# A hybrid decoder step on one Trainium2 core: gate temporaries beside the mixing get a buffer of their own, and the output projection's banks are copied before their squares are taken

## The chip, the cores and the metric

The kernel runs on one core of a Trainium2 chip. TensorE multiplies and writes its sums into banks of PSUM (512 fp32 columns on 128 partitions each); ScalarE (ACT), VectorE (DVE) and GpSimd (POOL) move and transform data between PSUM and SBUF; SyncE (SP) and ScalarE's queue issue the DMAs between SBUF and DRAM. Each engine runs its own instructions in order and waits on semaphores for the others. The metric is the device time of one execution in microseconds, and lower is better. The time before is the median of three runs.

## What is computed

One layer of a decoder, for a prompt of 1024 tokens and a sample group of 64 tokens (8 sequences of 8) that share the weights. Model width is 1024, the feed-forward width 2816:

```python
def swiglu(x, w_gu, w_down):
    g, u = jnp.split(x @ w_gu, 2, axis=-1)
    return (jax.nn.silu(g) * u) @ w_down
...
        x = x + 0.5 * rms_norm(swiglu(rms_norm(x, norm_ffn1_pre[l]), ffn1_w_gu[l], ffn1_w_down[l]),
                               norm_ffn1_post[l])
        h = rms_norm(x, norm_mix_pre[l])
        z = h @ w_in[l] + b_in[l]
        q, k, v, hq, hf, hi, hg = jnp.split(z, [int(c) for c in np.cumsum(IN_SPLITS)[:-1]], axis=-1)
...
        mix = jnp.concatenate([a, o], axis=-1) @ w_out[l]
        x = x + rms_norm(mix, norm_mix_post[l])
        x = x + 0.5 * rms_norm(swiglu(rms_norm(x, norm_ffn2_pre[l]), ffn2_w_gu[l], ffn2_w_down[l]),
                               norm_ffn2_post[l])
```

Here `a` is a windowed attention with sinks, normalised, and `o` a chunked gated linear recurrence (HGRN2), normalised and gated. So the order of the layer is: first FFN, mixing (input projection, attention and recurrence, output projection), second FFN.

## The kernel before

The 1088 tokens are split into three groups: group 0 with 320 columns (256 prompt tokens and the 64 sample tokens), groups 1 and 2 with 384 prompt tokens each. Every large product is made in three matmuls (`mm3`, L279 to L281) of operands split into a high and a low part: hi x hi, hi x lo, lo x hi. A weight tile is loaded into a `raw` slot (three of them), cast to its high part on ScalarE (L258, `wsph`) and subtracted to its low part on VectorE (L259, `wspl`); eight tiles of tag `wsp` hold four such pairs. Products go into `mm` banks (four), small ones of the mixing into `ax` banks (four).

The FFN for group 0 is done column tile by column tile. A unit (`up0`) makes the gate bank, 24 matmuls of 320 columns, and the up bank, 24 more. `gated0` copies the gate bank to a temporary (L676), applies Silu to it (L677), multiplies it by the up bank on VectorE (L680) and stores it to DRAM from SyncE's queue (L681). Before, this temporary is one of the eight tiles of tag `t2` (`tmp2`), 128 x 512 fp32 each, which rotate among all temporaries of the mixing (attention probabilities and their transposes, the recurrence's Q, K and D, gain rows, loaded residual rows).

The mixing is woven into the large products: `mixer(n)` is a generator, started as a stream, and each unit of a large product calls `tick()`, which advances the streams by their rates. Group 0 is ready for the second FFN first, so its units are placed among the rest: five head units at the end of group 1's mixing, then group 2's mixing starts, and beside it stand the output projection of group 1 and nine more head units; the output projection of group 2 follows. `need(name)` writes out what is left of a stream. Then eight more head units run, with the stream that adds the residual of group 2 (`post_n`) and prepares its FFN input (`pre_s`). The written order is not final: a scheduler with a time line of its own reorders each engine's instructions when the program is built, so that an instruction's place on its engine follows from when that time line has its inputs and buffers ready.

The output projection of groups 1 and 2 (`w_out_units`, the loop over two column halves `hf`) makes three banks of 128 tokens x 512 columns from four weight tiles. ScalarE then squares each bank with a sum along the row (for the norm, L1535) and copies it to `y` in SBUF (L1537); VectorE multiplies `y` in place by the gain row (L1539). A bank is free for the next product when its square and its copy are done. As each group has two halves, there are 12 squares and 12 copies in all.

Other lines that the prediction's steps touch: the mixing's transposes and products on TensorE are L1154, L1178, L1206, L1219 (attention), L1251, L1274, L1305, L1323, L1329, L1332, L1336 (recurrence); L1195 is the attention's exponential and L1325 the copy of the recurrence's transposed keys, both on ScalarE; L1239 copies K into a temporary; L1413 stores a piece of the sample group's attention; L1307, L1141 and L1142 form the last part of the mixing's output, whose high and low parts the output projection reads.

Of the kernel before, what the change touches and what calls it, by code (L numbers as in the profile page):

```python
# [8 lines left out]
F32 = mybir.dt.float32  # L9
# [4 lines left out]
AF = mybir.ActivationFunctionType  # L14
# [4 lines left out]
P = 128  # L19
D = 1024  # L20
# [17 lines left out]
Z_K, Z_V, Z_HQ, Z_HF, Z_HI, Z_HG = 4, 5, 6, 10, 14, 18  # L38
LEVELS = [64, 32, 16, 8, 4, 2, 1]
NRAW = 3  # L40
WARM = 23, 7
P1 = 1.4

# [2 lines left out]
def tile_step(ctx: ExitStack, tc: tile.TileContext, A: dict, O: list):  # L46
    nc = tc.nc
    V, S, G, PE = nc.vector, nc.scalar, nc.gpsimd, nc.tensor
# [8 lines left out]
    def uid(s):  # L57
        cnt[0] += 1
        return f"{s}_{cnt[0]}"

    def mmbank():
        return ps.tile([P, 512], F32, tag="mm", bufs=4, name=uid("mm"))
# [8 lines left out]
    def big(dt=F32, shape=(P, 4, 384)):  # L71
        return pp.tile(list(shape), dt, tag="big", bufs=12, name=uid("big"))
# [17 lines left out]
    def rawslot(shape=(P, KC, P)):  # L90
        return pp.tile(list(shape), F32, tag="raw", bufs=NRAW, name=uid("raw"))

# [4 lines left out]
    def stream(name, gen, rate):  # L97
        streams[name] = [gen, rate, 0.0]

    def tick():  # L100
        for name in list(streams):
            st = streams[name]
            st[2] += st[1]
            while st[2] >= 1.0:
                st[2] -= 1.0
                if next(st[0], "end") == "end":
                    del streams[name]
                    break
# [12 lines left out]
    junk = cp.tile([P, 512], BF16, name="junk")  # L121
# [132 lines left out]
    def small():  # L254
        return pp.tile([P, 4, 8], F32, tag="small", bufs=10, name=uid("sm"))
# [5 lines left out]
    def load_w(src, pool, tag, bufs, shape=(P, KC, P)):  # L261

        raw = rawslot(shape)
        for sl, ap in src:
            nc.sync.dma_start(raw if sl is None else raw[:, :, sl], ap)
        hi = pool.tile(list(shape), F32R, tag=tag, bufs=bufs, name=uid(tag + "h"))
        lo = pool.tile(list(shape), F32R, tag=tag, bufs=bufs, name=uid(tag + "l"))
        split(hi, lo, raw)
        return hi, lo
# [4 lines left out]
    def load_up(w, c0):  # L274
        return load_w([(None, wsrc(w, c0))], pp, "wsp", 8)
# [7 lines left out]
    def hcol(h, k, w):  # L283
        return h[0][k // 4][:, k % 4, :w], h[1][k // 4][:, k % 4, :w]

    def proj(out, wt, h, w, ks=range(KC)):
        for k in ks:
            mm3(out, (wt[0][:, k, :], wt[1][:, k, :]), hcol(h, k, w), k == 0, k == KC - 1)

    def proj_tok(banks, wt, h, n, ks):  # L290

        for i, bank in enumerate(banks):
            r = rows_of(n, i)
            for k2, k in enumerate(ks):
                hh = hcol(h, k, WIDTH[n])
                mm3(bank[:r], (hh[0][:, i * P:i * P + r], hh[1][:, i * P:i * P + r]),
                    (wt[0][:, k2], wt[1][:, k2]), k == 0, k == KC - 1)
# [8 lines left out]
    def tmp2(name, shape=(P, 512)):  # L306
        return pp.tile(list(shape), F32, tag="t2", bufs=8, name=uid(name))
# [96 lines left out]
    def gain_row(ap, scale, hf):  # L404
        g = tmp2("gb")
        nc.scalar.dma_start(g, ap[0:1, hf * 512:hf * 512 + 512].partition_broadcast(P))
        if scale is not None:
            V.tensor_scalar(g, g, scale, None, op0=ALU.mult)
        return g
# [146 lines left out]
    def pre_first(y, rows, gpre, h, raws, wts, part):  # L556
# [7 lines left out]
        def warm(n):  # L564
            for _ in range(n):
                last = PE.matmul(spare[:, :P], ones, ones, start=True, stop=True).ins
            return last

        last_tr = warm(WARM[0])
        V.memset(sm[:, 0, :], 1.0)  # L570
# [22 lines left out]
        for d in range(KC):  # L593
            bank = axbank("tr")
            with tc.issue_after(last_tr):
# [5 lines left out]
                if d == 1:  # L601
                    last_tr = warm(WARM[1])
            hi, lo = hcol(hx, d, w)
# [44 lines left out]

    def make_ffn(wgu, wdn, h, tag):
        f = FFN()  # L650
        f.SF, f.ys, f.pool = {}, {}, None
        acts = dr.tile([P, NJ, WIDTH[0]], F32, name=f"act{tag}")
        FA = dr.tile([P, NK, 7, 384], F32, name=f"fa{tag}")
        FB = dr.tile([P, NK, 4, 512], F32, name=f"fb{tag}")
# [16 lines left out]

        def gated0(j, g):
            w = WIDTH[0]
            t = tmp2("sg")

            S.copy(t[:, :w], g[:, :w])  # L676
            S.activation(t[:, :w], t[:, :w], AF.Silu)  # L677

            def rest(u):
                V.tensor_tensor(t[:, :w], t[:, :w], u[:, :w], op=ALU.mult)  # L680
                return nc.sync.dma_start(acts[:, j], t[:, :w]).ins  # L681
            return rest
# [360 lines left out]
    def mixing(tp, h):  # L1043
# [464 lines left out]
        def w_out_units(n, ys, sums):  # L1508
            w = WIDTH[n]
            if n == 0:  # L1510
                y = ys[n] = [big(), big()]
                for d in range(KC):
                    wt = load_up(w_out, d * P)
                    bank = mmbank()
                    proj(bank[:, :w], wt, MT[n], w, range(4))
                    tick()
                    proj(bank[:, :w], wt, MT[n], w, range(4, 8))
                    S.copy(y[d // 4][:, d % 4, :w], bank[:, :w])
                    tick()
                return  # L1520
            y = ys[n] = [big(F32, (P, 3, 512)), big(F32, (P, 3, 512))]
            sm = sums[n] = small()
            wts = Ahead([lambda kk=kk, hf=hf: load_w([(None, w_out[
                kk * 256:(kk + 1) * 256, hf * 512:hf * 512 + 512].rearrange("(k p) m -> p k m", p=P))],
                pp, "wsp", 8, (P, 2, 512)) for hf in range(2) for kk in range(4)])
            for hf in range(2):
                banks = [mmbank() for _ in range(3)]
                for kk in range(4):
                    wt = wts.next()
                    proj_tok(banks, wt, MT[n], n, (2 * kk, 2 * kk + 1))  # L1530
                    tick()
                    tick()
                g = gain_row(A["norm_mix_post"], None, hf)
                for i in range(3):
                    S.activation(junk, banks[i], AF.Square, scale=D ** -0.5,  # L1535
                                 accum_out=sm[:, 0, 4 * hf + i:4 * hf + i + 1])
                    S.copy(y[hf][:, i], banks[i])  # L1537
                for i in range(3):
                    V.tensor_tensor(y[hf][:, i], y[hf][:, i], g, op=ALU.mult)  # L1539

# [3 lines left out]
    def seq(*gens):  # L1544
        for g_ in gens:
            yield from g_
# [68 lines left out]
    f2 = make_ffn(A["ffn2_w_gu"][0], A["ffn2_w_down"][0], hffn2, 2)  # L1615
# [3 lines left out]
    def done_mix(n):  # L1619
        y, g = ym[n], cols[:, C_F2PRE:C_F2PRE + 8]  # L1620
        if n == 0:
            stream("c0", seq(post_t(y, x1T, cols[:, C_MPOST:C_MPOST + 8], x2T), pre_t(y, g, hffn2)), RB0)
        else:
            stream(f"c{n}", seq(post_n(n, y, sums[n], x1N[n - 1]),
                                pre_s(n, y, g, part, f2.SF, x2N[n - 1])), RB1)

    with tc.tile_pool(name="mx", bufs=1) as tp:
        w_in_units, mixer, w_out_units = mixing(tp, hmix)
        need("c0")
        w_in_units(0)  # L1630
        stream("m0", mixer(0), RM[0])
        half1(1)
        f1.pair(PB, False, last=lambda: f1.begin_pair((7,), False))
        done1(1)
        f1.pair((7,), False, last=lambda: f1.begin_pair((4,), False))
        half1(2)
        f1.pair((4,), False)
        done1(2)
        need("c1")
        w_in_units(1)  # L1640
        need("m0")
        stream("m1", mixer(1), RM[1])
        w_out_units(0, ym, sums)
        done_mix(0)
        need("c2")
        w_in_units(2)
        need("c0")
        f2.head(range(HEAD2[0]))
        need("m1")
        stream("m2", mixer(2), RM[2])  # L1650
        w_out_units(1, ym, sums)
        done_mix(1)
        f2.head(range(HEAD2[0], HEAD2[1]))
        need("c1")
        need("m2")
        w_out_units(2, ym, sums)
        done_mix(2)
    def out0():
        y = f2.ys[0]
        yield from post_t(y, x2T, halfpost[:, 8:16])  # L1660
        for i in range(3):
            r = rows_of(0, i)
            dst = O[0][0, i * P:(i + 1) * P] if r == P else O[1].rearrange("b t d -> (b t) d")
            for hf in range(2):
                bank = axbank("yo")
                for c in range(4):
                    PE.transpose(bank[:r, c * P:(c + 1) * P], y[hf][:, c, i * P:i * P + r], ident)
                o = tmp2("yo")
                S.copy(o[:r], bank[:r])
                nc.sync.dma_start(dst[:, hf * 512:hf * 512 + 512], o[:r])  # L1670
            yield
# [37 lines left out]
    with tc.tile_pool(name="f2", bufs=1) as tp:  # L1709
# [10 lines left out]
        y, sm = f2.ys[1], small()  # L1720
# [32 lines left out]
```

## Time and profile before

| | us |
|---|---|
| median of 3 runs | 1993.24 (1992.93 to 1993.47) |
| the profiled execution | 1993.22 |
| span of its instructions | 1991.5 |
| TensorE busy | 1978.7 |
| VectorE busy | 1406.9 |
| ScalarE busy | 949.0 |
| GpSimd busy | 178.0 |

An engine's busy time is the union of its instructions' spans; idle time of an engine is shown in square brackets in a timeline, with what released it. In a list of waits the three numbers are us in all, times, and the longest. In a list of groups they are the busy time, the mean ns of one and the idle time just before them. Matmuls overlap, so that TensorE's pace is read from the distance between starts, not from the length of one.

### The profile page before, as it was taken

The numbers are of one execution on the slowest core, as the hardware profiler recorded it, in microseconds if no ns is written. First come the engines' busy times: TensorE is split into PE (matmuls) and PEld (weight loads), VectorE is DVE, ScalarE is ACT, GpSimd is POOL, SyncE is SP. The second block draws the span as 40 slices with busy tenths as digits, with TensorE's granted clock in tenths as the row PEclk, the third lists the DMA queues.
The fourth block names the chain that finished last, engine by engine and source line by source line (L and its number), as shares of the span: only waits on it lengthen the run. The fifth ranks groups of instructions, "written<-read, shape, count | busy, mean of one in ns | idle before, by whom it ended". The sixth has DMA issues, their size and how long they took to land.

```text
span 1991.5 us, 34618 instructions
## 1 busy us (share of the span) xinstructions
PE 1978.7 (99%) x13331; PEld 1854.6 (93%) x13331; DVE 1406.9 (71%) x2595; ACT 949.0 (48%) x1736; POOL 178.0 (9%) x244
## 2 busy tenths in 40 slices
PE   9999999999999999999999999999999999999998
PEld 8999999999998987797999898989999999999886
DVE  7686767886558656777667756756887877655667
ACT  5753334444445444445344444756544444444453
POOL 0000000000004101211113311220000000000201
PEclk9999999999999999999999999999999999999999
DMA  8735555755677647766434343527565555677874
GB/s 230 225 107 186 175 170 177 232 196 192 228 243 212 182 138 236 251 169 181 128 104 132 92 138 107 177 90 237 165 210 191 197 183 193 209 232 232 291 262 140
DMA packets 377319, 370.31 MB, mean 186 GB/s; under 512 B 40546, under 2 KB 294321, under 8 KB 377137
## 3 DMA queue, kind: packets, MB, share of 16 engines
q1 hardware_dynamic: 371169, 357.21, 56.9%
q10 hardware_dynamic: 5984, 10.88, 1.6%
q8 instruction: 105, 1.72, 0.4%
q14 instruction: 61, 0.50, 0.1%
HBM read 284.31 MB, written 84.71 MB: 185 GB/s over the span
## 4 chain that ended last, share of the span: by engine, by line
PE 96%; DMA 1%; DVE 1%; ACT 1%; issue 0%; SPq 0%; DVEq 0%; ACTq 0%
PE mm L279 28%; PE mm L280 28%; PE mm L281 28%; PE pv L1219 1%; PE c L281 1%; PE c L279 1%; PE c L280 1%; PE sc L1178 1%; PE pT L1206 1%; PE tr L511 1%; DMA ar<-fa 1%; PE lv L1251 1%; PE l L1274 0%; DMA raw<-in_ffn_w_gu_dram 0%; DMA xt<-in_x_prompt_dram 0%; PE av L1329 0%
## 5 line engine op out<-in xcount | busy, mean ns | idle before, releaser
L279 PE MATMUL mm<-h,wsph 128*128 128x320 f32 (+1 forms) x1280 | 407.3, 319 | 0.0
L280 PE MATMUL mm<-h,wsph 128*128 128x320 f32 (+1 forms) x1280 | 405.3, 317 | 0.0
L281 PE MATMUL mm<-h,wspl 128*128 128x320 f32 (+1 forms) x1280 | 403.6, 317 | 0.0
L258 ACT CAST wsph<-raw 128x1024 fp32r<-128x1024 f32 x200 | 209.1, 1048 | 269.6 <-PE mm L280 213.7
L259 DVE TENSOR_TENSOR wspl<-raw,wsph 128x1024 fp32r<-128x1024 f32 x200 | 247.7, 1240 | 125.3 <-ACT wsph L258 120.7
L258 ACT CAST w<-raw 128x512 fp32r<-128x512 f32 (+1 forms) x218 | 160.3, 740 | 209.2 <-PE mm L280 111.9
L259 DVE TENSOR_TENSOR w<-raw,w 128x512 fp32r<-128x512 f32 (+1 forms) x218 | 185.8, 856 | 87.6 <-ACT w L258 87.1
L279 PEld LDWEIGHTS mm<-h,wsph 128*128 128x128 f32 x1280 | 240.2, 188 | 3.8 <-issue 2.8
L281 PEld LDWEIGHTS mm<-h,wspl 128*128 128x128 f32 x1280 | 239.9, 188 | 2.8 <-issue 2.3
L280 PEld LDWEIGHTS mm<-h,wsph 128*128 128x128 f32 x1280 | 240.5, 188 | 1.5 <-issue 1.1
L279 PE MATMUL mm<-h,w 128*128 128x384 f32 (+1 forms) x720 | 240.3, 335 | 0.6 <-ACT w L258 0.5
L280 PE MATMUL mm<-h,w 128*128 128x384 f32 (+1 forms) x720 | 240.7, 335 | 0.0
L281 PE MATMUL mm<-h,w 128*128 128x384 f32 (+1 forms) x720 | 235.4, 334 | 0.0
L279 PE MATMUL mm<-w,h 128*128 128x512 f32 x462 | 181.1, 395 | 0.6 <-DVE big L975 0.6
L280 PE MATMUL mm<-w,h 128*128 128x512 f32 x462 | 181.3, 392 | 0.0
L281 PE MATMUL mm<-w,h 128*128 128x512 f32 x462 | 179.8, 391 | 0.0
L280 PE MATMUL mm<-big,w 128*128 128x384 f32 x528 | 176.5, 334 | 0.0
L279 PE MATMUL mm<-big,w 128*128 128x384 f32 x528 | 176.3, 334 | 0.0
L281 PE MATMUL mm<-big,w 128*128 128x384 f32 x528 | 176.2, 334 | 0.0
L279 PEld LDWEIGHTS mm<-h,w 128*128 128x128 f32 x720 | 135.0, 188 | 1.3 <-ACT w L258 0.7
L280 PEld LDWEIGHTS mm<-h,w 128*128 128x128 f32 x720 | 135.1, 188 | 0.1
L281 PEld LDWEIGHTS mm<-h,w 128*128 128x128 f32 x720 | 134.7, 188 | 0.1
(363 smaller groups left out, 3576.0 us busy)
## 6 DMA issues: line engine op xcount, KB each, us to landing
raw<-in_ffn_w_gu_dram SPq DMA_DIRECT2D x156, 512.0 KB
raw<-in_ffn_w_down_dram SPq DMA_DIRECT2D x74, 512.0 KB
raw<-in_w_in_dram SPq DMA_DIRECT2D x54, 512.0 KB
ar<-fa SPq DMA_DIRECT2D x70, 384.0 KB
big<-in_ffn_w_down_dram SPq DMA_DIRECT2D x88, 256.0 KB
fb<-big SPq DMA_DIRECT2D x44, 512.0 KB
fa<-big SPq DMA_DIRECT2D x22, 768.0 KB
raw<-fb SPq DMA_DIRECT2D x30, 512.0 KB
```

Source lines behind the costliest of these rows:

```text
L258: S.copy(hi, src)
L259: (lo_eng or V).tensor_tensor(lo, src, hi.bitcast(F32), op=ALU.subtract)
L279: PE.matmul(out, a[0], b[0], start=first, stop=False, skip_group_check=resume)
L280: PE.matmul(out, a[0], b[1], start=False, stop=False, skip_group_check=resume)
L281: return PE.matmul(out, a[1], b[0], start=False, stop=last, skip_group_check=resume).ins
L511: PE.transpose(bank[:, i * P:(i + 1) * P], y[kh][:, i, k * P:(k + 1) * P], ident)
L1178: PE.matmul(banks[g][:, i * 256:i * 256 + wk], zq[64 * g:64 * g + 64, 2 * pr + i, b * P:(b + 1) * P], kx[64 * g:64 * g + 64, k0:k0 + wk], ...
L1206: PE.transpose(bank[:, (i * nk + kb) * P:(i * nk + kb + 1) * P], pt[g][:, i, kb * P:(kb + 1) * P], ident)
L1219: PE.matmul(ob[:, hd * 64:hd * 64 + 64], pT[g][:, (i * nk + kb) * P:(i * nk + kb + 1) * P], vn[:, vb, g * 64:g * 64 + 64], start=kb == 0, ...
L1251: PE.matmul(b5[cs, n_, a], x[:, a, cs], y[:, a, cs], start=True, stop=True)
```

## The change

Three places. A constant says how many buffers the new tag has:

```diff
+SIDE = 1
```

`gated0` takes its temporary from the FFN's `side` pool while there is one, with the unit's 320 columns, and from the shared `t2` ring otherwise. For the second FFN, `side` is the mixing's pool from the start of the mixing until the output projection of group 2 has been written out. So the five and the nine head units use the single buffer of tag `sg`, and every other unit the ring:

```diff
-        f.SF, f.ys, f.pool = {}, {}, None
+        f.SF, f.ys, f.pool, f.side = {}, {}, None, None
...
-            t = tmp2("sg")
+
+            t = f.side.tile([P, w], F32, tag="sg", bufs=SIDE, name=uid("sg")) if f.side else tmp2("sg")
...
     with tc.tile_pool(name="mx", bufs=1) as tp:
+        f2.side = tp
         w_in_units, mixer, w_out_units = mixing(tp, hmix)
...
         done_mix(2)
+        f2.side = None
+
```

In the output projection the three copies are written first, and the squares read the copies in SBUF in place of the banks:

```diff
                 for i in range(3):
-                    S.activation(junk, banks[i], AF.Square, scale=D ** -0.5,
+                    S.copy(y[hf][:, i], banks[i])
+                for i in range(3):
+                    S.activation(junk, y[hf][:, i], AF.Square, scale=D ** -0.5,
                                  accum_out=sm[:, 0, 4 * hf + i:4 * hf + i + 1])
-                    S.copy(y[hf][:, i], banks[i])
                 for i in range(3):
                     V.tensor_tensor(y[hf][:, i], y[hf][:, i], g, op=ALU.mult)
```

The scheduler then orders each engine's instructions anew. Up to the first head units, and again from a few units behind the output projection of group 2, the order stays as it was.

## The prediction

> **What bounds the kernel now.** I read the page first: busy time by engine, then the chain that ended last.
>
> ```profile
> span 1991.5 us, 34618 instructions
> ...
> PE 1978.7 (99%) x13331; PEld 1854.6 (93%) x13331; DVE 1406.9 (71%) x2595; ACT 949.0 (48%) x1736; POOL 178.0 (9%) x244
> ...
> PE 96%; DMA 1%; DVE 1%; ACT 1%; issue 0%; SPq 0%; DVEq 0%; ACTq 0%
> ```
>
> TensorE works for 1978.7 of 1991.5 us, and 96% of the chain is its own work. Neither edit adds or drops a matmul, so the most that can be won is TensorE's idle time, 12.8 us, and only the part of it that lies where the edits act. The list of TensorE's waits says what ended that idle time where a wait ended it:
>
> ```profile
> PE ax L566 <- DVE sm L570: 1.1, 1, 1.1
> PE lv L1251 <- DVE big L1369: 1.1, 1, 1.1
> PE tr L598 <- DMA big<-in_x_sample_dram: 0.8, 1, 0.8
> PE mm L279 <- ACT wsph L258: 0.6, 1, 0.6
> PE mm L279 <- DVE big L975: 0.6, 2, 0.4
> PE mm L279 <- ACT w L258: 0.5, 1, 0.5
> PE spv L1405 <- DVE t L1400: 0.4, 1, 0.4
> ```
>
> Next the stretch in which the edits act: the second FFN's head units and the last two output projections, with the start of what follows. The row gives window, length, then busy us of PE, PEld, DVE, ACT, POOL:
>
> ```profile
> 1130.00:1430.00 300.00, 299.36 (x2553) 276.32 (x2552) 201.69 (x415) 168.94 (x332) 37.58 (x65) 1.00 0.47 145
> ```
>
> TensorE idles 0.64 us in these 300, at a clock of 1.00. That is one wait: the L279 line for wsph above. TensorE's timeline shows its place, and ScalarE's shows what stood in front of the cast that ended it:
>
> ```profile
> 1344.46 0.39 PE L280 MATMUL mm<-wspl,h 128*128 128x512 f32 x1
> 1344.69 0.39 PE L281 MATMUL mm<-wsph,h 128*128 128x512 f32 x1
> 1345.71 0.96 PE L279 MATMUL mm<-wsph,h 128*128 128x512 f32 x3 [0.64 <-ACT wsph L258]
> ```
>
> ```profile
> 1342.47 0.61 ACT L1535 ACTIVATE junk<-mm 128x512 bf16<-128x512 f32 x1
> 1343.04 0.61 ACT L1537 COPY big<-mm 128x512 f32<-128x512 f32 x1
> 1343.50 0.64 ACT L1535 ACTIVATE junk<-mm 128x512 bf16<-128x512 f32 x1
> 1344.08 0.63 ACT L1537 COPY big<-mm 128x512 f32<-128x512 f32 x1
> 1344.55 1.11 ACT L258 CAST wsph<-raw 128x1024 fp32r<-128x1024 f32 x1
> ```
>
> In the last output projection, two squares and two copies ran back to back from 1342.47 to 1344.55, and the weight cast for the second column half stood behind them. From start to start TensorE lost 1.02 us where its step is 0.23, so 0.79 us.
>
> **Copies first, squares from the copies.** All of this is on ScalarE, and counts stay: 12 squares and 12 copies.
>
> ```profile
> L1535 ACT ACTIVATE junk<-mm 128x512 bf16<-128x512 f32 x12 | 7.2, 602 | 2.5 <-PE mm L281 2.4
> L1537 ACT COPY big<-mm 128x512 f32<-128x512 f32 x12 | 7.1, 589 | 0.0
> ```
>
> A bank was free after 602 + 589 ns and is free after 589. In the built program of the change, the first bank's copy stands before the casts for the second half, the second bank's copy behind both, and the squares later still. So of the 2.08 us in front of the cast at most one copy is left: it can start 1.5 us earlier, which is more than the 0.79 lost. I book **-0.79**; the other end is 0, if something else is late at that place (first rival). A square now reads SBUF, which no row here shows for this form; between the copy's 589 ns and the weight cast's rate (1024 columns in 1050 ns, below, so 525 ns for 512) it would gain 77 ns, and 12 of them 0.9 us, all on an engine that is idle for half the span. I take 0.
>
> The multiplies of L1539 work in place, so they now wait for the squares too. Behind them on VectorE stand weight splits (L259). In the built order the third multiply comes only after the splits for the next three weight tiles, so nothing that TensorE needs soon is queued behind it. I book 0; without that cover it is one square, 0.6 us.
>
> **Gate temporaries in a place of their own.** Fourteen gate units run beside the mixing (five, then nine). Their rows in the same window, which holds 22 units, and the weight cast's row:
>
> ```profile
> L258 ACT CAST wsph<-raw 128x1024 fp32r<-128x1024 f32 x58 | 60.6, 1050 | 70.6 <-PE mm L280 70.1 <-PE mm L281 0.5
> ...
> L680 DVE TENSOR_TENSOR sg<-sg,mm 128x320 f32<-128x320 f32 x22 | 10.7, 484 | 15.3 <-ACT sg L677 7.5 <-PE mm L281 7.2 <-issue 0.5
> L677 ACT ACTIVATE sg<-sg 128x320 f32<-128x320 f32 x22 | 10.4, 470 | 0.3
> L676 ACT COPY sg<-mm 128x320 f32<-128x320 f32 x22 | 9.2, 421 | 0.8 <-DVE big L439 0.6 <-issue 0.2
> ```
>
> Copy, Silu and product keep their 421, 470 and 484 ns. What changes is when the copy may start: not after the eighth tile back in the shared ring, but after the store of the unit just before, because there is one buffer. The copy can move forward, and the scheduler does move it: in the built order a unit's copy mostly stands one to three weight casts earlier, and stores stand earlier on SyncE past one or two weight loads. Freeing the gate's bank sooner wins nothing, since TensorE has no wait for a bank in this window.
>
> The new wait needs a price. TensorE's step for a 320-wide matmul is 0.146 us, and a bank takes 24 of them:
>
> ```profile
> 1153.67 0.39 PE L1332 MATMUL av<-st,t 128*128 128x128 f32 x2
> 1153.81 0.39 PE L281 MATMUL mm<-h,wspl 128*128 128x320 f32 x1
> 1154.04 0.30 PE L279 MATMUL mm<-h,wsph 128*128 128x320 f32 x1
> 1154.19 0.31 PE L280 MATMUL mm<-h,wsph 128*128 128x320 f32 x1
> 1154.33 0.30 PE L281 MATMUL mm<-h,wspl 128*128 128x320 f32 x1
> ```
>
> So the next gate is complete 24 x 0.146 = 3.5 us after the up bank or later, and after the product's 0.48 the store has 3.0 us to land before the next copy is held. This store's landing stands in no row. The nearest is a small store from a shared tile, whose release ScalarE waited for:
>
> ```profile
> 868.28 0.53 SPq L1413 DMA_DIRECT2D osc<-t  x1
> ...
> 873.51 0.41 ACT L1239 COPY t<-big 128x256 f32<-128x256 f32 x1 [5.24 <-DMA osc<-t]
> ```
>
> That is 5.2 us, so a copy is held between 0 and 2.2 us. [...]
>
> Behind a held copy on ScalarE stand the Silu, weight casts and the mixing's copies and exponentials. The casts have cover: the 58 of them waited 70.6 us for TensorE to free their tile, and a tile freed now is needed after three others have been used, 3 x 3.5 = 10.5 us, against 1.05 of cast and 1.24 of split. The mixing has less. Its tightest link that I found is TensorE's transpose, ScalarE's copy and TensorE's next use:
>
> ```profile
> 1339.03 0.60 PE L1323 MATMUL kT<-ident,t 128*128 128x128 f32 x4
> 1339.66 0.59 ACT L1325 COPY t<-kT 128x512 f32<-128x512 f32 x1 [3.02 <-PE kT L1323]
> 1341.25 0.94 PE L1336 MATMUL u<-big,t 128*128 128x128 f32 x7
> ```
>
> The copy ends at 1340.25 and is used at 1341.25: 1.0 us to spare. I take 0 for the wait, since twelve units have the mixing's own matmuls between them and so more than 3.5 us; its upper end is the second rival.
>
> Two more activation tables are loaded, because Silu and exponential alternate more often; such a load has a row:
>
> ```profile
> L1195 ACT ACT_TABLE_LOAD x4 | 5.1, 1283 | 0.1
> ```
>
> 2 x 1.283 us fall on ScalarE, which is busy for 169 of the 300 us; 0 on TensorE, and up to 2.6 if both stood ahead of a late cast.
>
> **The order on TensorE.** The scheduler places the mixing's small matmuls anew. In the stretch that holds everything that moves (from the second FFN's first head units to the head units behind the last output projection), the built orders have 49 blocks of small matmuls among the large ones before and 43 after, and 74 against 81 changes of tile inside blocks. The timeline above prices a block: after the av block the first step is 0.23 instead of 0.146, so 0.085 us. Six blocks less win 0.5 us; seven changes more cost between 0 and 7 x 0.085 = 0.6. Between -0.5 and +0.1 I take **-0.2**.
>
> **Sum.** The profiled execution took 1993.22 us (span 1991.5 and 1.7 around it), 0.02 from the median of 1993.24. 1993.22 - 0.79 - 0.2 = **1992.2 us**; by the ends of the terms 1991.9 to 1993.3.
>
> **Rivals.**
> First, the wait comes back a few tiles later. In the built order, the last recurrent block's final transposes stand 45 large matmuls later than before, and 12 instead of 29 large ones (12 x 0.23 = 2.8 us) remain until TensorE needs the result. That result passes VectorE and ScalarE, 0.7 and 0.6 us for 512 columns; with one weight split of 1.24 us ahead the slack is about gone, with two it is 1.1 us late: 1992.2 + 1.1 = 1993.3, no change. For it: the order is tight there. Against: the split that could stand ahead belongs to a cast that is released 13 matmuls before the transposes.
>
> Second, slower: the store of the single buffer lands late. Each held copy can cost TensorE 2.2 - 1.0 = 1.2 us, and it decides from a landing of 3.0 + 1.0 = 4.0 us after the product. Three hits give 1992.2 + 3.6 = 1995.8, all twelve 2006.6. For it: SyncE issues in order, and its weight loads wait in front of stores:
>
> ```profile
> SPq L265 <- DVE wspl L259: 408.2, 128, 9.4
> ...
> SPq L681 <- DVE sg L680: 97.0, 27, 13.0
> ```
>
> Against: the second row says that SyncE mostly stands at the store and waits for the product, so the store leaves at once. [...]
>
> Third, a larger gain: the 0.085 us after each block is really a short wait for ScalarE or VectorE, and earlier evictions remove it: 49 x 0.085 = 4.2, so 1988.2 us. Against: it is nearly constant, and the waits name none of it.
>
> **How the numbers follow.** Forecast 0.57, first rival 0.26, second 0.13, third 0.04. The likeliest gives 1992.2. The range runs from 1990.9 (a block's 0.085 counted at both its sides, 6 x 0.17 = 1.0, for 1991.4, less the 0.5 us by which the runs before differ) to 1996.0, the second rival with three hits; it leaves out most of the second and the third, about 0.13. About 0.2%, 4.0 us, is what a measurement of this kernel can tell from no change. Faster by more is the third rival, 0.04; slower by more is the second with four hits or more, 0.09; the rest, 0.87, is within.
>
> **What would show it.** Right: TensorE's wait for wsph at the last output projection is gone, the window's idle time is near 0, gate copies start within 0.2 us of their bank, and everything behind ends about 1 us earlier. First rival: a wait for h (L1141, L1142) or for wsph shortly behind the hT transposes. Second: ScalarE's gate copy shows idle time ended by the store act<-sg, and TensorE waits for a mixing tile. Third: steps of 0.146 straight behind blocks. The forecast is wrong if TensorE's idle time in these 300 us exceeds 3 us.

## The result, and the profile after

| | before | after |
|---|---|---|
| median of 20 runs, us | 1993.09 (1990.73 to 1995.93) | 1996.69 (1995.67 to 1998.16) |
| profiled execution, us | 1993.22 | 1996.7 |
| its span, us | 1991.5 | 1994.9 |
| mean granted clock | 0.999 | 0.997 |

The ratio is 1.0019, with a 95% interval from 1.0013 to 1.0025: the change makes the kernel 3.6 us slower by the medians. The forecast was 1992.2 us, and its range ended at 1996.0.

In the trace of after, the line numbers behind L40 are one higher, those from L676 on two higher and those behind L1536 three to six higher than before. The list of what TensorE waited for (us in all, times, longest):

```profile
PE pv L1221 <- DVE t L1211: 2.6, 1, 2.6
PE ax L567 <- DVE sm L571: 1.1, 1, 1.1
PE lv L1253 <- DVE big L1371: 0.8, 1, 0.8
PE spv L1407 <- DVE t L1402: 0.2, 1, 0.2
PE mm L280 <- DVE big L977: 0.2, 1, 0.2
```

The wait for `wsph` is gone, as forecast. A wait of 2.6 us is new: the attention's product (`pv`) of group 2 waits for the transposed probabilities, which VectorE copies at L1211 (L1209 before). The row of the 300 us in which the edits act (window, length, busy us of PE, PEld, DVE, ACT, POOL, then the clock):

```profile
1130.00:1430.00 300.00, 297.42 (x2528) 274.97 (x2527) 201.06 (x410) 170.12 (x328) 35.35 (x65) 0.99 0.47 143
```

TensorE idles 2.58 us here, against 0.64. These 1.9 us more do not make up the loss of 3.5 us between the two profiled executions. The clock column shows more lost time in this execution: 0.99 over 300 us. Three rows around the wait, each with TensorE's busy time and its clock:

```profile
1250.00:1256.56 6.56, 4.07 (x58) 1.00 0.71 238
1256.56:1263.40 6.84, 6.75 (x28) 0.50 0.55 148
1263.40:1270.00 6.60, 6.60 (x103) 1.00 0.98 350
```

For 6.84 us behind the wait the granted clock was 0.50. TensorE's timeline shows the wait, the slow steps and the return:

```profile
1253.61 0.46 PE L1253 MATMUL ld<-t,t 128*32 128x32 f32 x32
1256.65 2.19 PE L1221 MATMUL pv<-vn,t 128*128 128x64 f32 x9 [2.58 <-DVE t L1211]
...
1262.63 0.47 PE L282 MATMUL mm<-h,wspl 128*128 128x320 f32 x1
1262.90 0.47 PE L280 MATMUL mm<-h,wsph 128*128 128x320 f32 x1
1263.16 0.42 PE L281 MATMUL mm<-h,wsph 128*128 128x320 f32 x1
1263.42 0.31 PE L282 MATMUL mm<-h,wspl 128*128 128x320 f32 x1
1263.56 0.31 PE L280 MATMUL mm<-h,wsph 128*128 128x320 f32 x1
```

From start to start a 320-wide matmul takes 0.27 us there and 0.14 to 0.15 behind 1263.4. Half of 6.84 us, 3.42, is lost in steps that count as busy. So 2.58 + 3.42 = 6.0 us are lost in this execution in place of 0.64. Of this excess of 5.4 the two executions differ by only 3.5: in after, the first head unit already starts 1.2 us sooner, in a part that the edits do not touch, and 0.7 us are left over, which the order on TensorE may have won; they were not traced. The half clock is taken up again under the experiments, since an execution can be as late without it. The two starts, before and after:

```profile
1140.54 0.39 PE L279 MATMUL mm<-h,wsph 128*128 128x320 f32 x1
```

```profile
1139.33 0.39 PE L280 MATMUL mm<-h,wsph 128*128 128x320 f32 x1
```

Where the wait comes from is read backwards. VectorE's timeline of after:

```profile
1248.92 1.22 DVE L260 TENSOR_TENSOR wspl<-raw,wsph 128x1024 fp32r<-128x1024 f32 x1 [0.45 <-ACT wsph L259]
...
1251.43 0.72 DVE L1144 TENSOR_TENSOR h<-t,h 128x512 fp32r<-128x512 f32 x1
1255.24 0.75 DVE L440 SCALAR_TENSOR_TENSOR big<-big,sm,xt 128x512 f32<-128x512 f32 x1 [3.09 <-DMA xt<-x1N]
1255.91 0.68 DVE L1211 COPY t<-pT 128x512 f32<-128x512 f32 x1
```

The copy of the probabilities stands behind the residual step of group 1 (L440, L439 before), and that step waited 3.09 us for its row `xt` to be loaded. The same copy and the same product before:

```profile
1254.52 0.68 DVE L1209 COPY t<-pT 128x512 f32<-128x512 f32 x1
```

```profile
1255.80 1.89 PE L1219 MATMUL pv<-vn,t 128*128 128x64 f32 x16
```

Counted from the first head unit, the copy ends at 114.7 us before and at 117.3 after, and TensorE gets to the product at 115.3 before and at 114.7 after. So it is the copy that is late; the order on TensorE moved the product by only some half a us. The issuing engine's timeline says why the row came late; SyncE before, then after:

```profile
1245.65 1.97 SPq L427 DMA_DIRECT2D xt<-x1N  x4
1248.81 0.38 SPq L265 DMA_DIRECT2D raw<-in_ffn_w_gu_dram  x1
1250.63 0.32 SPq L681 DMA_DIRECT2D act<-sg  x1
```

```profile
1240.21 3.80 SPq L266 DMA_DIRECT2D raw<-in_ffn_w_gu_dram  x2
1248.50 0.34 SPq L683 DMA_DIRECT2D act<-sg  x1
1250.17 0.37 SPq L266 DMA_DIRECT2D raw<-in_ffn_w_gu_dram  x1
1250.63 1.96 SPq L428 DMA_DIRECT2D xt<-x1N  x4
```

Before, the four residual loads went out first. After, a gate store and a weight load stand ahead of them, and they go out at 1250.63 in place of 1245.65, or 6.2 us later counted from the first head unit. The store left at 1248.50, when its product was done; the weight load left at 1250.17, just after the split of 1248.92 (1.22 us long) had freed its `raw` slot. Two instructions ahead of the loads could each be what held them; the experiments had to tell which.

The hold that the prediction had feared is nearly absent. In the view of the tile `sg` from 1120 to 1365, the gate copies' idle time that a store ended (us, times) is:

```profile
  DMA act<-sg: 1.0, 1
```

The store that held this copy was issued at 1261.31, and the copy started at 1268.30, so the store took up to 7.0 us. The other copies, the nearest of them 3.7 us behind the store before it, were not held.

### The profile page after: what moved, and what is told of

The parts are those of the page before. It is cut to its first block, busy times and chain, and to the rows that moved or that the text cites. A ratio compares the mean times of both kernels' runs of the same rounds, so it can differ in the third digit from the quotient of the medians.

```text
span 1994.9 us, 34626 instructions
## 1 busy us (share of the span) xinstructions
PE 1982.5 (99%) x13331; PEld 1859.0 (93%) x13331; DVE 1411.1 (71%) x2595; ACT 953.8 (48%) x1738; POOL 174.1 (9%) x244
## 4 chain that ended last, share of the span: by engine, by line
PE 96%; DMA 1%; DVE 1%; ACT 1%; issue 0%; DVEq 0%; POOL 0%; SPq 0%; ACTq 0%; POOLq 0%
PE mm L280 28%; PE mm L282 28%; PE mm L281 28%; PE pv L1221 1%; PE c L280 1%; PE c L282 1%; PE c L281 1%; PE sc L1180 1%; PE pT L1208 1%; PE lv L1253 1%; PE tr L512 1%; DMA ar<-fa 1%; PE ax L567 1%; DMA xt<-in_x_prompt_dram 0%; PE l L1276 0%; PE av L1331 0%
```

## The experiments

In their traces the line numbers are those of before, or a few off. All times are medians; each ratio is against runs of the kernel before on the same chip, whose medians lie between 1992.22 and 1993.09 us, so kernels that ran on different chips are compared by their ratios. `issue_after` puts an instruction behind another one on its engine.

**One edit at a time.** First the gate buffer without the copies-first order:

```diff
                 for i in range(3):
                     S.activation(junk, banks[i], AF.Square, scale=D ** -0.5,
...
                     S.copy(y[hf][:, i], banks[i])
```

> The gate temporaries' own buffer alone; squares and copies as before. Theory (ring): with the gate temporaries out of the shared ring the order on SyncE becomes that of the change, a gate store and a weight load ahead of the four residual loads xt<-x1N; VectorE's residual step waits for them, a pT copy of the attention takes the ring slot of the first residual tile, and TensorE waits at pv near 1254 us. In this built order VectorE's pT copy stands ahead of the residual step, ScalarE's still needs its slot, so the wait should shrink from 2.6 to 1 to 1.8 us; if the clock is halved behind it again, +3.4 us, so 1995.5 to 1996.5, if not, 1992 to 1993.5. Rival (squares): the loss comes from squares that read SBUF and from the multiplies that wait for them, so this kernel is at 1992 to 1993 without a wait at pv.

It took 1999.39 us, ratio 1.0032 (1.0020 to 1.0045), about 3 us above the expected 1995.5 to 1996.5. So the gate buffer alone brings the whole loss. Two rows of TensorE's timeline show the wait at `pv` and one at a bank of the last output projection:

```profile
1257.75 0.47 PE L1219 MATMUL pv<-vn,t 128*128 128x64 f32 x1 [1.40 <-ACT t L1209]
...
1354.85 0.50 PE L279 MATMUL mm<-wsph,h 128*128 128x512 f32 x1 [1.45 <-ACT big L1537]
```

The first is the wait that was expected, 1.40 us where 1 to 1.8 were. VectorE's copy stands ahead of the residual step here. What `pv` waits for is the other copy of the probabilities, on ScalarE, and that one waited for the residual step:

```profile
1257.11 0.59 ACT L1209 COPY t<-pT 128x512 f32<-128x512 f32 x1 [2.46 <-DVE big L439]
```

The copy writes a tile of the shared ring, which also holds the residual rows until the residual step has read them. In the change ScalarE's copy waits in the same way, for 2.34 us. So late residual loads reach `pv` on two ways, by VectorE's order and by the ring.

The second wait, which was not expected, is for ScalarE's copy of the bank, behind squares. With both edits it is gone, and the ratio is 1.0019 (1.0013 to 1.0025) in place of 1.0032; as the two intervals overlap, a gain in time is not shown.

Then the copies-first order alone, with `t = tmp2("sg")` as before:

```diff
+                    S.copy(y[hf][:, i], banks[i])
+                for i in range(3):
+                    S.activation(junk, y[hf][:, i], AF.Square, scale=D ** -0.5,
```

> Copies first and squares from the copies alone; gate temporaries in the ring. Theory (ring): orders on SyncE and VectorE near 1250 us are those of before, no wait at pv, no half clock; the 0.6 us wait for wsph at the last output projection is gone: 1992.0 to 1993.0, about 0.8 below before. Rival (squares): about 1996 to 1997 as the change.

It took 1991.37 us, ratio 0.9992 (0.9983 to 1.0), a little below the expected 1992.0 to 1993.0. TensorE's row of the 300 us:

```profile
1130.00:1430.00 300.00, 299.55 (x2556) 276.96 (x2555) 203.38 (x417) 170.76 (x333) 38.05 (x65) 1.00 0.48 147
```

No wait for `wsph` and a whole clock. Because the interval touched 1, the same kernel ran again:

> The copies-first edit alone once more, because its first interval (0.9983 to 1.0) reached no difference. If the removed 0.8 us wait and the 0.6 us that this trace gained from the first head unit beside the mixing to the end of the last output projection are all there is, the ratio is 0.9996 (0.8/1993) to 0.9993; if the 1.3 us of the first comparison is real, 0.9990 to 0.9994. No difference or slower would mean that the first result was chance.

1991.9 us, ratio 0.9998 (0.9989 to 1.0007). In this profile, too, the wait was gone, and TensorE's 300 us held no idle time (300.00 busy, clock 1.00). The wait is removed, then, but a gain of 0.8 us in the whole time is below what these runs can tell. It is the fastest of the versions tried.

**The order on SyncE.** The change, with the gate store and the weight load put behind the residual loads:

```diff
-            nc.sync.dma_start(raw if sl is None else raw[:, :, sl], ap)
+            with behind(1940 < cnt[0] < 1950): nc.sync.dma_start(raw if sl is None else raw[:, :, sl], ap)
...
-                return nc.sync.dma_start(acts[:, j], t[:, :w]).ins
+                with behind(f.side and j == 6): return nc.sync.dma_start(acts[:, j], t[:, :w]).ins
```

Here `behind` is an `issue_after` of the last of the four residual loads, and the two conditions pick one weight load and one store.

> The change, with one gate store and one weight load put behind the residual loads xt<-x1N on SyncE, as before the change. Theory (ring): the loads are issued near 1245 instead of 1250.6 us, VectorE's residual step does not wait 3 us, TensorE's wait at pv is under 1 us and the clock stays at 1.00: 1991.5 to 1993.0. Rival (single buffer: what costs is the gate copy held by its own store): the wait stays, 1996 to 1997.

It took 1993.19 us, ratio 1.0003 (0.9995 to 1.0012). SyncE's timeline:

```profile
1242.22 1.96 SPq L427 DMA_DIRECT2D xt<-x1N  x4
1246.62 0.32 SPq L680 DMA_DIRECT2D act<-sg  x1
1248.29 0.38 SPq L265 DMA_DIRECT2D raw<-in_ffn_w_gu_dram  x1
```

TensorE's list of waits has at this place

```profile
PE pv L1218 <- ACT t L1208: 0.5, 1, 0.5
```

and the clock was 1.00 throughout the 300 us. With the loads first, most of the loss is undone: 3.6 us above before have become 0.6 (1993.19 against 1992.64 on the same chip). Which of the two instructions was it? First the store alone, sent through another engine's queue:

```diff
-                return nc.sync.dma_start(acts[:, j], t[:, :w]).ins
+                return (nc.gpsimd if f.side and j == 6 else nc.sync).dma_start(acts[:, j], t[:, :w]).ins
```

> One gate store (the unit whose store stood on SyncE at 1248.50, ahead of the first residual loads) is issued by GpSimd instead; the order on TensorE, VectorE and ScalarE is the change's own. Theory A (the store is what holds the residual loads): they go out 1.6 to 2 us earlier, TensorE's wait at pv falls from 2.6 to under 1 us, and the time falls to 1991.5 to 1995. Theory B (the weight load between the store and the residual loads holds them, because its raw buffer is freed by a split at 1250.14, and the store only stands in front of that): nothing moves; the residual loads still go out at about 1250.6 (as counted in the change's trace), the pv wait stays 2.6 us, the clock is halved again, and the time stays within 1 us of the change's 1996.7.

It took 1996.28 us, ratio 1.0020 (1.0011 to 1.0029): nothing gained. SyncE's timeline and, behind it, TensorE's wait:

```profile
1241.31 10.33 SPq L265 DMA_DIRECT2D raw<-in_ffn_w_gu_dram  x3
1251.73 1.96 SPq L427 DMA_DIRECT2D xt<-x1N  x4
```

```profile
PE pv L1219 <- DVE t L1209: 2.8, 1, 2.8
```

The store no longer stands there, and the loads are as late as ever, behind the third weight load of the 10.33 us stretch: 111.3 us behind the first head unit, as in the change. So taking away the store alone frees nothing. Now the weight load alone, put behind the residual loads, with the store left where it was:

```diff
-            nc.sync.dma_start(raw if sl is None else raw[:, :, sl], ap)
+            with behind(1940 < cnt[0] < 1950): nc.sync.dma_start(raw if sl is None else raw[:, :, sl], ap)
```

> Only the weight load that stood between the gate store and the first residual loads on SyncE is put behind those four loads; the gate store stays ahead of them. Theory B (the weight load holds them): the residual loads go out at 1248.9 instead of 1250.6, the pv wait falls from 2.6 to 0.9 us or less, the clock is not halved there, and the time comes to 1991.5 to 1994. Theory A (the store holds them): no change against the change's 1996.7, or slower because the weight tile comes later.

It took 1993.97 us, ratio 1.0008 (0.9999 to 1.0017). SyncE, then VectorE, then TensorE's wait:

```profile
1248.64 0.34 SPq L680 DMA_DIRECT2D act<-sg  x1
1249.08 2.00 SPq L427 DMA_DIRECT2D xt<-x1N  x4
1251.18 0.38 SPq L265 DMA_DIRECT2D raw<-in_ffn_w_gu_dram  x1
```

```profile
1252.22 1.44 DVE L438 SCALAR_TENSOR_TENSOR big<-big,sm,xt 128x512 f32<-128x512 f32 x2
1253.58 0.68 DVE L1208 COPY t<-pT 128x512 f32<-128x512 f32 x1
```

```profile
PE pv L1218 <- ACT t L1208: 0.3, 1, 0.3
```

The residual step starts at 1252.22 with no wait for its row, the wait at `pv` falls to 0.3 us, and no stretch at half clock follows: the 300 us have a clock of 1.00. Against the run with the store through GpSimd, on the same chip, the median is 2.3 us lower. The copy starts 114.1 us behind the first head unit, as before (114.0), and not at 116.6 as in the change. So one weight load, moved ahead of the residual loads, makes up most of the loss, together with what the scheduler orders anew because of it: in this run two residual steps stand ahead of the copy, in the change one.

The load made the rows late by more than its place in the order. In the change the four loads go out 1.7 us later (111.3 against 109.6 us behind the first head unit), and the residual step starts 4.6 us behind the first of them, where 3.1 us were enough here. What makes that second part was not shown; the weight load ahead of the rows moves 512 KB (by the page of after), and its share was not tried by itself.

**The half clock.** Does it cost time of its own? The change with twelve matmuls of ones into the `pv` bank ahead of the waiting `pv` keeps TensorE busy there:

```diff
+                with tc.issue_after(ldl[-1]):
+                    for _ in range(NFILL): last = PE.matmul(ob[:, :P], ones, ones, start=True, stop=True).ins
```

> The change, with twelve 128-column matmuls of ones into the pv bank (overwritten by pv) right ahead of the pv that waits, about 2.6 us of TensorE work in place of the idle time. Theory (clock): TensorE isn't idle there, the granted clock stays at 1.00 through 1250 to 1270 us, and the 6.8 us at half clock (3.4 us lost) are gone although pv starts no earlier: 1992.5 to 1994. Rival (the clock record follows something else, or half clock costs nothing because other work sets the pace): 1996 to 1997 as the change.

It took 2002.67 us, ratio 1.0049 (1.0035 to 1.0062), a plain miss. The clock stayed whole in the profile, but new waits came:

```profile
1130.00:1430.00 300.00, 294.19 (x2530) 271.40 (x2529) 196.60 (x404) 169.08 (x326) 35.35 (x65) 1.00 0.46 140
```

```profile
PE lv L1257 <- DVE t L1291: 4.5, 2, 2.7
PE tr L511 <- DVE big L493: 1.2, 1, 1.2
```

This run changed two things: with the longer filling, the scheduler also moved a block of small matmuls (`lv`) from 24 large matmuls behind `pv` to straight behind it. A second one therefore used four matmuls, which moves that block by seven and leaves SyncE's order as it is in the change (`NFILL = 4`):

> The change with four matmuls of ones into the pv bank in front of the waiting pv, so that TensorE idles some 1.7 us there instead of 2.6; the orders on SyncE and VectorE stay, and on TensorE one block of small matmuls behind the wait comes seven large matmuls earlier. If the halved clock behind the wait costs time of its own (3.4 us of lost steps): the clock stays whole and the time falls by 2 to 3.5 us against the change, to 1993 to 1995. If VectorE and the late residual step set the pace there anyway: the clock stays whole, TensorE waits instead at the next blocks of small matmuls, and the time stays at 1996 to 1998.

1998.15 us, ratio 1.0028 (1.0017 to 1.0039). The wait at `pv` and the clock behind it:

```profile
1255.40 2.00 PE L1223 MATMUL pv<-vn,t 128*128 128x64 f32 x16 [1.62 <-DVE t L1213]
```

```profile
1257.50:1260.90 3.40, 3.40 (x15) 3.40 (x14) 3.23 (x7) 1.90 (x6) 0.00 (x0) 0.50 0.75 186
1260.90:1264.00 3.10, 3.10 (x51) 2.49 (x51) 0.75 (x1) 0.45 (x1) 0.74 (x1) 1.00 1.01 368
```

Half the stretch at half clock, 1.7 us of steps won back, and no time won; both readings had expected a whole clock. A table of all profiles for the same 300 us, with the idle time from such window rows and half the length of the stretch at clock 0.50:

| kernel | idle, us | lost at half clock, us | matmuls of ones, us | median, us (ratio) |
|---|---|---|---|---|
| copies-first alone (two profiles) | 0.45, 0.00 | 0 | 0 | 1991.37, 1991.9 (0.9992, 0.9998) |
| before | 0.64 | 0 | 0 | 1993.09 |
| both put behind the residual loads | 1.67 | 0 | 0 | 1993.19 (1.0003) |
| weight load behind them | 1.32 | 0 | 0 | 1993.97 (1.0008) |
| store through GpSimd | 2.79 | 3.4 | 0 | 1996.28 (1.0020) |
| the change | 2.58 | 3.4 | 0 | 1996.69 (1.0019) |
| four matmuls of ones | 3.92 | 1.7 | 1.2 | 1998.15 (1.0028) |
| gate buffer alone | 3.70 | 3.4 | 0 | 1999.39 (1.0032) |
| twelve matmuls of ones | 5.81 | 0 | 2.8 | 2002.67 (1.0049) |

Idle time and clock are those of one profiled execution, which need not be like the median one: with twelve matmuls of ones it took 2000.48 us at a mean clock of 0.999, and the four others took 2000.84 to 2003.61 at 0.996 to 0.998.

Among the kernels with the gate buffer, only those that brought the residual loads forward got rid of the half clock and of the lost time together. Where it was taken away by work in the gap, other waits for VectorE grew by more. One reading is that the mixing's chain was behind by then, so that a faster TensorE would only have waited; but both fillers also moved small matmuls.

The mean clock of every execution speaks for that reading. A stretch of 6.84 us at half clock takes 3.42 of 1995 us, or 0.0017, off the mean. Of the 31 executions of the change and of the store through GpSimd, 15 had a mean of 0.997, as the two profiled ones, 13 had 0.998 and 3 had 0.999, which leaves at most 3.0 us of lost steps and so no room for such a stretch. Their median times are 1996.7, 1996.3 and 1996.2 us, and the three still took 2.6 to 3.7 us more than the median of before on their chip. So in these three most of the loss is there without the long stretch. They were not profiled, so how TensorE waited in them is not known, and what the half clock costs by itself stays open.

## Why the prediction was wrong

**Right: the copies first, -0.79.** The `wsph` wait at the last output projection is gone in the change and in both profiles of that edit alone. The first rival (the wait comes back behind the `hT` transposes) did not show: no wait for `h` or `wsph` is in the list. In the whole time the 0.79 us could not be told from nothing. The wait of 1.45 us for a bank of that stage, which the gate buffer alone has, is also gone with both edits.

**Right in effect, wrong in sign: the squares from SBUF.** I expected up to 77 ns less for each and booked 0, and I wrote that no row shows a square that reads SBUF. The kernel before has that form in another norm, L394, with 36 squares of 629 ns on average. In the change, a square takes 631 ns where it took 602:

```profile
L1539 ACT ACTIVATE junk<-big 128x512 bf16<-128x512 f32 x12 | 7.6, 631 | 0.2
```

No wait of TensorE follows from it.

**Wrong: the gate temporaries, booked at 0.** The step that failed is the sentence that "stores stand earlier on SyncE past one or two weight loads", which I left without a price, so that the term stood at 0. I priced only what a late store does to the next gate copy. I did not list what else had changed places on SyncE: four residual loads now stood behind a weight load whose `raw` slot was freed at 1250.14. Behind those loads stood the residual step on VectorE, behind that the copy of the transposed probabilities, and for that copy TensorE waited 2.58 us. Putting the one load back behind them took away 2.3 of the 3.6 us. Each link lies in the order of one engine or in the shared ring, and the built order had the swap in it before any run.

The hold that I did price at 0 to 2.2 us came once, with 1.0 us, and the list of TensorE's waits names none for `sg`. The store that held it took up to 7.0 us, more than the 5.2 us of the row that I had taken as nearest. No run shows a store that lands within the 3.0 us to spare; the nearest copy that was not held started 3.7 us behind the store before it (1170.10 against 1166.40).

What makes the slot late is visible but was not tried by itself. ScalarE's timeline of after shows the gate's Silu between the exponentials and the cast that the split waited for:

```profile
1246.19 1.28 ACT L679 ACT_TABLE_LOAD   x1
1247.48 0.47 ACT L679 ACTIVATE sg<-sg 128x320 f32<-128x320 f32 x1
1247.86 1.03 ACT L259 CAST wsph<-raw 128x1024 fp32r<-128x1024 f32 x1
```

Table load, Silu, cast: with its weights landed, the cast could have started 1.67 us sooner without the first two. I had given table loads a price of up to 2.6 us "if both stood ahead of a late cast" and taken 0. Why the scheduler put the weight load ahead of the residual loads stays open.

**Wrong: the second rival's place.** It had the right sign, engine and nearly the right price (1995.8 with three hits), by a mechanism that did not occur: one copy was held, for 1.0 us. That its price came out near is luck. What it cited for itself, that SyncE issues in order, was the true cause (the residual loads left at 1250.63, behind the weight load at 1250.17) with other parts in it: not a store held by a product, as the run without that store shows, but a load held by a weight slot.

**The order on TensorE, -0.2.** In the account of the two profiled executions, 0.7 us in after's favour remain for it and all else; the sign fits, and no run separates it.

**The bound that I had set on idle time was blind to it.** The forecast was to be wrong if TensorE idled over 3 us in the 300. It idled 2.58, and the forecast was wrong. The 3.4 us in slow steps are busy time, so idle time alone was the wrong test for this execution; the clock column belonged beside it.

**Open.** With the residual loads first, the gate buffer is still 1.8 us behind the copies-first edit alone on the same chip (1993.19 against 1991.37). Part is idle time (1.67 us in the 300, against 0.45), in small waits at `pv`, `lv` and `tr`; the rest was not traced.

## What to carry to other kernels

When a scheduler reorders the program, compare the built orders of every queue, SyncE's first, and follow what now stands behind a moved DMA until it reaches the bounding engine; an instruction that carries none of the change's data can carry its cost. When two instructions stand ahead of a late one, move them one at a time: the one that the change names (the store) was not the one that held it. Read idle time and granted clock together, because steps at half clock are counted as busy (6.75 us of the 6.84 at clock 0.50 in the change).

## What was unexpected of the hardware

I had not looked for a halved clock behind waits of 1.4 to 2.8 us, and length alone does not decide. It fell to 0.50 behind, or towards the end of, waits of 1.40 us (gate buffer alone), 1.62 (four matmuls of ones), 2.58 (the change) and 2.79 us (store through GpSimd; the row from 1254.00 to 1257.95, which holds the wait, has 0.89, and the 6.80 us behind it have 0.56). It stayed whole through a wait of 2.73 us in the profiled execution with twelve matmuls of ones, in a window in which TensorE was busy for 1.27 of 4 us, and through the 1.1 us wait at `lv` of the kernel before (1.00 from 755 to 768 us, around the wait that ended at 758.12). One kernel can do either: the means of the change's 20 executions run from 0.997 to 0.999. The row of that window of the twelve-matmul run:

```profile
1264.00:1268.00 4.00, 1.27 (x20) 1.04 (x22) 2.04 (x4) 1.41 (x4) 0.00 (x0) 1.00 0.75 284
```

The halved stretch lasted 6.84 us in the change, 6.80 with the gate buffer alone (1257.70 to 1264.50, clock 0.50) and 3.40 in the run with four matmuls of ones. What decides whether the clock is halved, and for how long, no run shows: 1.40 us of waiting went with a halved clock in one execution, and 2.73 us with a whole one in another.
